# Query and key projections as 512-column products, and thirteen low parts by DMAs issued with their negation

## The chip, the cores and the metric

The kernel runs on one core of one Trainium2 chip. The core has TensorE (PE in the profile; PEld is its weight load), VectorE (DVE), ScalarE (ACT), GpSimd (POOL) and the queues that issue DMAs, above all SyncE's (SP) and GpSimd's. The metric is the device time of one execution in microseconds; of several runs the median counts.

## The reference

One layer of a hybrid decoder trunk on 256 rows of width 1024, in float32:

```python
n = _rmsnorm(h, norm_mix_g[l])
z = n @ w_in[l]
c_a, c_g, q, k, v, qi, ki, wi, gc_logit, ga_logit = _split_cols(z, IN_SIZES)
g_conv = jax.nn.sigmoid(gc_logit + bg_conv)
g_attn = jax.nn.sigmoid(ga_logit + bg_attn)
y_conv = _conformer_conv(c_a, c_g, conv_w[l], conv_b[l], conv_ln_g[l], conv_ln_b[l], w_conv_out[l])
y_attn = _dsa_attention(qh, kh, vh, qih, ki, wih) @ w_attn_out[l]
h = h + (g_conv * y_conv + g_attn * y_attn) @ w_mix_out[l]
h = h + _cross_attention(_rmsnorm(h, norm_x_g[l]), _rmsnorm(mem, norm_mem_g[l]), wx_q[l], wx_kv[l], wx_o[l])
hf = _rmsnorm(h, norm_ffn_g[l]) @ w_ff1[l]
h = h + jnp.square(jax.nn.relu(hf)) @ w_ff2[l]
return _rmsnorm(h, norm_final_g)
```

`_conformer_conv` multiplies one projection by the sigmoid of another, convolves each of 1024 channels with 31 causal taps, applies layer norm and silu, and projects. `_dsa_attention` has 8 heads of 128; an indexer of 8 small heads picks 64 keys for each query.

## The kernel before, in words

**Precision.** Each float32 operand is split into a high part, rounded to the matmul's type fp32r, and a low part, the rest. A product is made of three: high with high, high with low, low with high. For the weights the split happens in the kernel: a chunk `raw` of 128 x 2048 is loaded by SP, ScalarE copies each half (128 x 1024) to `hi`, and VectorE subtracts to give `lo`. For some second halves the low part is made otherwise: ScalarE writes minus `hi` into `lo`, and a DMA issued by POOL adds `raw` to it (`low_by_dma`, line 181).

**The stream.** The list `STREAM` fixes the order in which weight chunks are loaded and used: conv 0 to 3, the indexer's qi and ki, conv 4 to 7 (chunks 7 to 10), the gates gc and ga (11 to 18), v (19 to 22), q and k in turn (23 to 30), xk and xv of the cross attention (31 to 34), then ao (attention output, 35 to 38), co (conv output), mix, xq, xo, and the feed-forward f1 and f2. There are six buffers each of `hi` and `lo` and three of `raw`.

**Half tiles.** `form_b` handles one chunk as two half tiles of 128 output channels. A half tile has 8 steps over the input. In the narrow form a step is three products of 256 columns. In the wide form (`is_wide`, line 287) the high part of the weights multiplies both parts of the rows at once, 512 columns, and the low part multiplies the high rows, 256 columns, into the second half of the same PSUM bank; the two halves have to be added at the end. `merge` (line 319) does this: ScalarE copies the second half out, VectorE adds the first. `copy_out` (line 329) is a plain copy on ScalarE for a narrow half tile and a merge for a wide one: at once for k (`now=True`), as a chain for the others.

**Chains, ticks, fill.** Work beside the products is written as Python generators. `tick()`, called after each half tile, moves every started chain on by one `yield`, so a `yield` puts the next part of a chain behind the next half tile in the engines' orders. The 31 taps of each of 8 conv channel tiles (`acc`) wait in the list `fill`; `tick` emits taps as long as the planned cost of VectorE's work is more than 1000 below the planned cost of PE's. So what else VectorE is given in a stage sets how many taps stand there.

**The norm of the conv branch.** When all taps of all 8 tiles are emitted, `layer_norm` (line 622) is started. POOL adds up the tiles (`usum`). PE forms the mean (`ps_mub`), VectorE subtracts it, ScalarE squares, PE and POOL make the reciprocal root (`ps_vr`, `rs_vr`, `ps_rsb`), and then, pair by pair of channel tiles, VectorE scales, ScalarE applies silu, and VectorE splits into `u_p`, one pair for a tick. Before the co products, `finish(norms[0])` drains what is left. The co products read `u_p`.

**Heads.** A head's chain (`head`, line 667) begins one tick after its k half tile: scores `ps_s` on PE, mask and maximum `att_t` on VectorE, exponential on ScalarE, transposes `ps_pt` and output `ps_o` on PE, split into `o_p`.

Of the kernel before, what the change touches and what calls it, by code (L numbers as in the profile page):

```python
# [8 lines left out]
F32 = mybir.dt.float32  # L9
# [3 lines left out]
ALU = mybir.AluOpType  # L13
# [20 lines left out]
STREAM = (  # L34
    [("conv", i) for i in range(4)]
    + [("qi", i) for i in range(2)]
    + [("ki", 0)]
    + [("conv", i) for i in range(4, 8)]
    + [("gc", i) for i in range(4)]
    + [("ga", i) for i in range(4)]  # L40
    + [("v", i) for i in range(4)]
    + [(n, i) for i in range(4) for n in ("q", "k")]
# [69 lines left out]
def block_kernel(ctx, tc, x, xt, mem, memt, wst, wki, vecs, convw, gout, out):  # L112
    nc = tc.nc
# [14 lines left out]
    def t8(name, dt=F32, shape=(P, KT, S)):  # L128
        return big.tile(list(shape), dt, tag="t8", bufs=12, name=name)

    def parts_t8(name, nkt=KT):
        return Parts([t8(f"{name}{c}", F32R, (P, 4, 2, S)) for c in range(nkt // 4)])

    def w2(name, dt=F32, shape=(P, 512)):
        return work.tile(list(shape), dt, tag="w2", bufs=8, name=name)
# [10 lines left out]
    def ps_aux(name):  # L146
        return bank("aux", 2, name)
# [13 lines left out]
    def load(parts=1):  # L161
        if nload[0] >= len(STREAM):
            return
        c = nload[0]
        nload[0] += 1
        key = STREAM[c]
        raw = t8(f"raw{c}", F32, (P, N_CHUNK)) if c in EARLY else raws.tile([P, N_CHUNK], F32, tag="raw", name=f"raw{c}")
        n = KT * NK if key[0] == "ki" else N_CHUNK
        src = wki if key[0] == "ki" else wst[INDEX[key]]
        for q in range(parts):  # L170
            ns = slice(q * n // parts, (q + 1) * n // parts)
            nc.sync.dma_start(raw[:, ns], src[:, ns])
        if key in WHOLE:
            whole[key] = raw.rearrange("p (k n) -> p k n", k=2 * KT)
            return
        parts = 1 if key[0] == "ki" else 2
        for q in range(parts):
            ns = slice(q * n // parts, (q + 1) * n // parts)
            high_jobs.append(lambda ns=ns, q=q, last=q == parts - 1: high(key, c, raw, ns, q, last))

    def low_by_dma(key, c, q):

        return q == 1 and c % 3 == 2 and 8 <= c < STREAM.index(("ao", 1))

    def high(key, c, raw, ns, q, last):
        n = ns.stop - ns.start
        hi = highs.tile([P, N_CHUNK // 2], F32R, tag="hi", name=f"hi{c}_{q}")[:, :n]
        lo = lows.tile([P, N_CHUNK // 2], F32R, tag="lo", name=f"lo{c}_{q}")[:, :n]
        act(hi, raw[:, ns], AF.Copy)  # L189
        by_dma = low_by_dma(key, c, q)  # L190
        if by_dma:
            act(lo, hi.bitcast(F32), AF.Copy, scale=-1.0)

        def low():
            if by_dma:
                nc.gpsimd.dma_start(lo.bitcast(F32), raw[:, ns], accum_op=ALU.add)
            else:
                dve.tensor_tensor(out=lo, in0=raw[:, ns], in1=hi.bitcast(F32), op=ALU.subtract)
            prepared[(*key, q)] = (hi, lo)
            if last and c not in EARLY:  # L200
                load()

        low_jobs.append(low)
# [82 lines left out]

    def is_wide(kind, ct):

        return kind in ("f1", "gc", "ga", "ao", "xk") or (kind == "mix" and ct < 6) or (kind == "co" and ct < 6)

    def form_b(kind, i, x2, after, ps_of=ps_mm):

        for ct in range(2):
            w = weights(kind, i, ct, KT)
            split_ahead()
            ps = ps_of(f"ps_{kind}{i}{ct}")
            wide = is_wide(kind, 2 * i + ct)
            tile_b(ps, w, x2, wide=wide)
            after(2 * i + ct, ps if wide else ps[:, :S])
            tick()  # L300

    def form_b_late(kind, i, x2, after, cuts=(KT - 1,), ps_of=None):

        ws, banks = [], []
        held[0] = 2
        for ct in range(2):
            ws.append(weights(kind, i, ct, KT))
            split_ahead()
            banks.append((ps_of or ps_mm)(f"ps_{kind}{i}{ct}"))
            tile_b(banks[ct], ws[ct], x2, range(cuts[0]), is_wide(kind, 2 * i + ct))  # L310
        for lo, hi in zip(cuts, (*cuts[1:], KT)):
            for ct in range(2):
                tile_b(banks[ct], ws[ct], x2, range(lo, hi), is_wide(kind, 2 * i + ct))
        for ct in range(2):
            after(2 * i + ct, banks[ct] if is_wide(kind, 2 * i + ct) else banks[ct][:, :S])
            tick()
        held[0] = 1
# [64 lines left out]
    def rsqrt(sums, name):  # L382

        ps = ps_aux(f"ps_{name}")
        for rb in range(2):
            pe.matmul(ps[:, 2 * rb : 2 * rb + 2], sums[:, rb * P : rb * P + P], onesd[:, :2], start=True, stop=True)
        ms = small.tile([P, 2], F32, tag="ms", name=f"ms_{name}")
        dve.tensor_scalar(ms, ps[:, :4].rearrange("p (r t) -> p r t", r=2)[:, :, 0], EPS, None, ALU.add)
        return power(ms, name)

    def spread(cols, name):

        ps = ps_aux(f"ps_{name}")
        for rb in range(2):
            pe.transpose(ps[:, rb * P : rb * P + P], cols[:, rb : rb + 1].to_broadcast([P, P]), ident)
        return ps[:, :S]
# [65 lines left out]
    def tap(t, s):  # L462
        def go():
            j = TAPS - 1 - s
            if s == 0:
                act(acc[:, t, :], u[:, t, :], AF.Identity, scale=cw[:, t, j : j + 1], bias=cvb[:, t : t + 1])
            else:
                dve.scalar_tensor_tensor(out=acc[:, t, s:], in0=u[:, t, : S - s], scalar=cw[:, t, j : j + 1],
                                         in1=acc[:, t, s:], op0=ALU.mult, op1=ALU.add)
            if s == TAPS - 1:  # L470
                done.append(t)
                if len(done) == KT:
                    norms.append(start(layer_norm()))
                if len(done) > 1:
                    nc.gpsimd.tensor_tensor(out=usum, in0=usum if len(done) > 2 else acc[:, done[0], :],
                                            in1=acc[:, t, :], op=ALU.add)
        return go
# [143 lines left out]

    def layer_norm():
        u2.append(parts_t8("u_p"))
        yield
        mub = ps_aux("ps_mub")[:, :S]
        pe.matmul(mub, onesd, usum, start=True, stop=True)
        mub = mub.unsqueeze(1).to_broadcast([P, 2, S])
        vs = w2("vs", F32, (P, 2, S))
        pairs = [slice(2 * c, 2 * c + 2) for c in range(4)]
        for c, cs in enumerate(pairs):  # L630
            dve.tensor_tensor(out=acc[:, cs, :], in0=acc[:, cs, :], in1=mub, op=ALU.subtract)
            sq = vs if c == 0 else w2(f"sq_vr{c}", F32, (P, 2, S))
            act(sq, acc[:, cs, :], AF.Square)
            if c > 1:
                dve.tensor_tensor(out=vs, in0=vs, in1=before, op=ALU.add)
            before = sq
        waiting[0] = True
        yield
        waiting[0] = False
        dve.tensor_tensor(out=vs, in0=vs, in1=before, op=ALU.add)  # L640
        dve.tensor_tensor(out=vs[:, 0, :], in0=vs[:, 0, :], in1=vs[:, 1, :], op=ALU.add)
        yield
        rs = rsqrt(vs[:, 0, :], "vr")
        yield
        while len(headed) < NH:
            yield
        act(table, table, AF.Silu)
        rsb = spread(rs, "rsb").unsqueeze(1).to_broadcast([P, 2, S])
        for c in range(5):
            if c < 4:  # L650
                dve.tensor_tensor(out=acc[:, pairs[c], :], in0=acc[:, pairs[c], :], in1=rsb, op=ALU.mult)
                for t in (2 * c, 2 * c + 1):
                    act(acc[:, t, :], acc[:, t, :], AF.Silu, scale=lng[:, t : t + 1], bias=lnb[:, t : t + 1])
            if c > 0:
                parts_of(2 * c - 2)
            yield

    def parts_of(kt):
        hi, src = u2[0].high(kt, 2), acc[:, kt : kt + 2, :]
        dve.tensor_copy(hi, src)  # L660
        dve.tensor_tensor(out=u2[0].low(kt, 2), in0=src, in1=hi.bitcast(F32), op=ALU.subtract)
# [44 lines left out]
    def qk(name):  # L706
        return big.tile([P, 2, S], F32, tag="qk", bufs=4, name=name)

    for i in range(4):
        q, k = qk(f"q{i}"), qk(f"k{i}")  # L710
# [441 lines left out]
```

## Time and profile before

| | us |
|---|---|
| median of 3 runs (515.99 to 517.21) | 516.72 |
| the profiled execution | 516.69 |
| its span, first to last instruction | 514.9 |
| busy: PE, DVE, ACT, POOL | 503.6, 421.6, 305.3, 27.8 |

The profile is one execution. PE's busy time counts matmuls that overlap as one stretch, so it does not say how fast the stream of products runs: for that, the time of a known number of products is read from the chain of waits. Almost all PE and DVE instructions are recorded at line 77 (a helper that counts cost), so groups are told apart by their tiles: `lo<-raw,hi` is a low part, `acc<-u,cw,acc` a tap, `ps_q`, `ps_k` and so on the half tiles. The TensorE clock granted was 0.998 on the mean.

### The profile page before, as it was taken

The numbers are of one execution on the slowest core, as the hardware profiler recorded it, in microseconds if no ns is written. First come the engines' busy times: TensorE is split into PE (matmuls) and PEld (weight loads), VectorE is DVE, ScalarE is ACT, GpSimd is POOL, SyncE is SP. The second block draws the span as 40 slices with busy tenths as digits, with TensorE's granted clock in tenths as the row PEclk, the third lists the DMA queues.
The fourth block names the chain that finished last, engine by engine and source line by source line (L and its number), as shares of the span: only waits on it lengthen the run. The fifth ranks groups of instructions, "written<-read, shape, count | busy, mean of one in ns | idle before, by whom it ended". The sixth has DMA issues, their size and how long they took to land.

```text
span 514.9 us, 8076 instructions
## 1 busy us (share of the span) xinstructions
PE 503.6 (98%) x3098; PEld 448.6 (87%) x3098; DVE 421.6 (82%) x822; ACT 305.3 (59%) x523; POOL 27.8 (5%) x40
## 2 busy tenths in 40 slices
PE   8999999999999999999999999999999999999995
PEld 6999998888899999888788998988888888888884
DVE  4998999999988999999989976796766566666565
ACT  5667666677556766748557657565644454544442
POOL 2001011101021000030000000000000000000000
PEclk9999999999999999999999999999999999999999
DMA  8946555766964644464646442546445554455402
GB/s 306 367 180 237 167 169 197 253 205 204 286 241 129 204 165 129 168 188 172 241 169 240 169 164 87 200 166 243 164 174 224 215 204 163 165 176 215 182 0 81
DMA packets 15750, 97.97 MB, mean 190 GB/s; under 512 B 1744, under 2 KB 2640, under 8 KB 5216
## 3 DMA queue, kind: packets, MB, share of 16 engines
q1 hardware_dynamic: 13952, 91.85, 48.7%
q0 software_dynamic: 1472, 5.28, 5.3%
q8 instruction: 24, 0.39, 0.3%
q10 hardware_dynamic: 288, 0.33, 0.2%
q14 instruction: 14, 0.11, 0.1%
HBM read 91.16 MB, written 1.05 MB: 179 GB/s over the span
## 4 chain that ended last, share of the span: by engine, by line
PE 74%; issue 10%; DVE 9%; DMA 4%; ACT 1%; POOL 1%; SPq 0%; POOLq 0%; DVEq 0%; ACTq 0%
PE ps_f L77 17%; PE ps_ff L77 16%; PE ps_k L77 4%; PE ps_q L77 4%; PE ps_mix L77 4%; PE ps_ga L77 4%; PE ps_v L77 4%; PE ps_co L77 4%; PE ps_conv L77 3%; DVE acc L77 3%; DVE lo L77 3%; PE ps_xo L77 3%; DMA raw<-in_wst_dram 2%; PE ps_xq L77 2%; PE ps_qi L77 2%
## 5 line engine op out<-in xcount | busy, mean ns | idle before, releaser
L77 DVE TENSOR_TENSOR lo<-raw,hi 128x1024 fp32r<-128x1024 f32 x153 | 184.9, 1220 | 3.7 <-ACT hi L189 2.2
L189 ACT ACTIVATE hi<-raw 128x1024 fp32r<-128x1024 f32 x163 | 168.6, 1047 | 5.2 <-DMA raw<-in_wst_dram 3.7
L77 DVE SCALAR_TENSOR_TENSOR acc<-u,cw,acc 128x235 f32<-128x235 f32 (+22 forms) x240 | 99.9, 472 | 0.5
L77 PE MATMUL ps_f<-ff_p,hi 128*128 128x512 f32 x256 | 89.9, 396 | 0.0
L77 PE MATMUL ps_ff<-hi,fs 128*128 128x512 f32 (+1 forms) x256 | 80.8, 387 | 0.0
L77 PE MATMUL ps_f<-ff_p,lo 128*128 128x256 f32 x256 | 66.2, 279 | 0.0
L77 PEld LDWEIGHTS ps_ff<-hi,fs 128*128 128x128 f32 x256 | 47.9, 188 | 9.2
L77 PEld LDWEIGHTS ps_f<-ff_p,hi 128*128 128x128 f32 x256 | 46.8, 188 | 9.2
L983 ACT ACTIVATE ft<-ps_f 128x256 f32<-128x256 f32 x32 | 12.2, 382 | 66.9 <-PE ps_f L77 66.9
L77 DVE TENSOR_TENSOR ft<-ps_f,ft 128x256 f32<-128x256 f32 x32 | 13.6, 424 | 45.8 <-ACT ft L983 45.8
L77 PEld LDWEIGHTS ps_f<-ff_p,lo 128*128 128x128 f32 x256 | 48.3, 189 | 2.6
L77 PE MATMUL ps_ff<-lo,fs 128*128 128x512 f32 (+1 forms) x128 | 49.4, 386 | 0.0
L77 PE MATMUL ps_conv<-n_p,hi 128*128 128x256 f32 x224 | 40.9, 285 | 0.4 <-ACT sg L494 0.4
L77 PEld LDWEIGHTS ps_conv<-n_p,hi 128*128 128x128 f32 x224 | 34.8, 191 | 1.6 <-ACT sg L494 0.8
L77 PE MATMUL ps_conv<-n_p,lo 128*128 128x256 f32 x112 | 31.7, 283 | 0.0
L77 PEld LDWEIGHTS ps_ff<-lo,fs 128*128 128x128 f32 x128 | 24.1, 188 | 4.9
L77 PE MATMUL ps_q<-n_p,hi 128*128 128x256 f32 x128 | 24.4, 291 | 0.0
L77 PE MATMUL ps_k<-n_p,hi 128*128 128x256 f32 x128 | 23.4, 284 | 0.0
L77 PE MATMUL ps_ao<-o_p,hi 128*128 128x512 f32 x64 | 22.8, 402 | 0.0
L77 PE MATMUL ps_co<-u_p,hi 128*128 128x512 f32 (+1 forms) x80 | 22.3, 351 | 0.3 <-DVE u_p L77 0.3
L77 PE MATMUL ps_mix<-mix_p,hi 128*128 128x512 f32 (+1 forms) x80 | 22.2, 351 | 0.0
L77 PE MATMUL ps_gc<-n_p,hi 128*128 128x512 f32 x64 | 22.0, 396 | 0.0
(238 smaller groups left out, 1008.5 us busy)
## 6 DMA issues: line engine op xcount, KB each, us to landing
raw<-in_wst_dram SPq DMA_DIRECT2D x80, 1024.0 KB, 4.9
lo<-raw POOLq DMA_DIRECT2D x10, 512.0 KB, 5.8
raw<-in_wst_dram SPq DMA_DIRECT2D x4, 512.0 KB, 8.9
x_rm<-in_x_dram SPq DMA_DIRECT2D x2, 512.0 KB, 3.8
mem_rm<-in_mem_dram SPq DMA_DIRECT2D x1, 1024.0 KB, 8.4
mem_t<-in_memt_dram SPq DMA_DIRECT2D x1, 1024.0 KB, 10.3
h_t<-in_xt_dram SPq DMA_DIRECT2D x1, 1024.0 KB, 7.0
out_dram<-hg SPq DMA_DIRECT2D x4, 176.0 KB, 2.1
```

Source lines behind the costliest of these rows:

```text
L77: return fn(*args, **kwargs)
L189: act(hi, raw[:, ns], AF.Copy)
L983: act(t, ps[:, S:], AF.Copy)
```

## The change

Four edits. `is_wide` now also takes q and k, so their sixteen half tiles are of the wide form and go through `merge`. `low_by_dma` takes every even chunk from 8 to 32 instead of every third from 8 to 35: thirteen second halves instead of ten. The DMA that completes a low part is issued right after its negation, in `high`, and no longer when the turn of the low part comes, in `low`. And `layer_norm` has one more `yield` ahead of the mean product.

```diff
     def low_by_dma(key, c, q):
 
-        return q == 1 and c % 3 == 2 and 8 <= c < STREAM.index(("ao", 1))
+        return q == 1 and c % 2 == 0 and 8 <= c < 34
 
     def high(key, c, raw, ns, q, last):
...
         if by_dma:
             act(lo, hi.bitcast(F32), AF.Copy, scale=-1.0)
+            nc.gpsimd.dma_start(lo.bitcast(F32), raw[:, ns], accum_op=ALU.add)
 
         def low():
-            if by_dma:
-                nc.gpsimd.dma_start(lo.bitcast(F32), raw[:, ns], accum_op=ALU.add)
-            else:
+            if not by_dma:
                 dve.tensor_tensor(out=lo, in0=raw[:, ns], in1=hi.bitcast(F32), op=ALU.subtract)
...
     def is_wide(kind, ct):
 
-        return kind in ("f1", "gc", "ga", "ao", "xk") or (kind == "mix" and ct < 6) or (kind == "co" and ct < 6)
+        return kind in ("f1", "gc", "ga", "ao", "xk", "q", "k") or (kind in ("mix", "co") and ct < 6)
...
     def layer_norm():
         u2.append(parts_t8("u_p"))
         yield
+        yield
         mub = ps_aux("ps_mub")[:, :S]
```

The last line of `is_wide` is otherwise the same rule for mix and co. The names `u_p`, `ya`, `ga_t` in VectorE's order keep their meaning; the lines behind the edited places move up by one.

## The prediction

> **What bounds the kernel now.** I read the page's shares first, then the busy time by stretches, then the chain of waits, and last the waits and single rows at the places where the chain changes engine.
>
> ```profile
> PE 503.6 (98%) x3098; PEld 448.6 (87%) x3098; DVE 421.6 (82%) x822; ACT 305.3 (59%) x523; POOL 27.8 (5%) x40
> ...
> 142.90:202.50 59.60, 59.60 (x482) 58.79 (x481) 54.21 (x139) 39.97 (x86) 6.86 (x6) 1.00 0.58 186
> 202.50:227.50 25.00, 24.77 (x136) 21.14 (x134) 24.75 (x56) 16.15 (x32) 4.86 (x4) 1.00 0.47 148
> 227.50:252.00 24.50, 23.60 (x133) 20.09 (x133) 23.92 (x41) 18.54 (x31) 0.72 (x1) 1.00 0.47 175
> 252.00:272.80 20.80, 20.78 (x132) 18.66 (x132) 18.64 (x35) 9.47 (x18) 0.00 (x0) 1.00 0.59 226
> ```
>
> The columns after the window are its length and then PE, PEld, DVE, ACT, POOL. TensorE looks like the bound everywhere (98%). But from 202.5 to 252.0 VectorE is just as full (24.75 of 25.00, 23.92 of 24.50), and two full engines in one stretch do not tell which one sets the end. The chain does:
>
> ```profile
> 201.78 0.67 PE ps_s L77 x4
> 202.47 0.29 DVE att_t L77
> ...
> 203.32 3.39 DVE acc L77 x9
> 206.71 1.14 DVE lo L77
> ...
> 245.38 0.34 DVE ya L77
> 245.75 0.43 DVE ga_t L77
> ...
> 251.27 0.70 DVE u_p L77
> ...
> 252.02 20.74 PE ps_co L77 x131
> 272.76 22.93 PE ps_mix L77 x144
> ```
>
> It runs on PE until the scores of head 7 (201.78), changes to VectorE at 202.47, stays there for almost fifty microseconds (conv taps `acc`, low parts `lo`, merges `ya`, gates `ga_t`, layer norm) and returns to PE only when the last `u_p` of the layer norm is written, at 251.97. The wait behind it is in the rows:
>
> ```profile
> 251.29 0.38 PE L77 MATMUL ps_co<-u_p,lo 128*128 128x256 f32 x1 [0.56 <-DVE u_p L77]
> 252.02 0.73 PE L77 MATMUL ps_co<-u_p,hi 128*128 128x512 f32 x2 [0.34 <-DVE u_p L77]
> ...
> DVE att_t L77 <- PE ps_s L77: 3.9, 2, 2.5
> ```
>
> PE idles 0.90 us for `u_p`. Ahead of the attention VectorE was early: it waited 3.9 us for the scores of heads 0 and 1. So the rule for this change: before head 7, what PE saves counts; from head 7 to the last `u_p`, every instruction added on VectorE counts; after it PE counts again (20.78 busy of 20.80).
>
> **The change part by part.**
>
> *Wide products on PE.* The sixteen half tiles of q and k turn from 24 products of 256 columns into 8 of 512 and 8 of 256.
>
> ```profile
> 98.93 22.39 PE ps_ga L77 x128
> ...
> 148.85 5.76 PE ps_k L77 x48
> ```
>
> Two narrow half tiles of k took 5.76, so 2.88 each. Eight wide ones of the attention gate took 22.39, so 2.80 each, small waits included. 16 x 0.08 = **-1.3 us**, all but the last of it ahead of head 7's scores.
>
> The Trainium skill, *TensorE: Matmul & The Clock Gate*, section Back-to-back issue gap, gives N / 2.4 GHz plus about 2.5 ns from one warm matmul to the next. By it a narrow half tile would be 2.62 us and a wide one 2.60, the gain an estimated 0.3 us and the sum below 1.0 later. The trace differs: 5.76 us for 48 narrow products is 120 ns each, not 109, so the row is used.
>
> *Merges on VectorE.* A wide half tile needs its two halves added. ScalarE's copy is there in both forms, so each of the sixteen adds one VectorE addition. The nearest kind is the `ya` merge of the chain above: 0.34 in a busy stretch (its own duration is 0.42, but the next instruction starts before it ends). 16 x 0.34 = +5.4.
>
> *Low parts by DMA.* Ten become thirteen, so three subtractions leave VectorE: 3 x 1.14 = -3.4. ScalarE gets three negations, 3 x 1.06 = 3.2, in stages where it has room (39.97 busy of 59.60 in the q and k window); were that cover gone, it would be at most 3.2. VectorE's net is **+2.0** over the kernel. Where it falls decides, and that is in the order: `low_by_dma` no longer takes chunk 35, so its second half comes back to VectorE behind head 7. Counted in VectorE's order from head 7's `att_t` to the last `u_p`, the change has 37 taps for 35, 14 low parts for 13, 8 `ya` for 6 and 8 `ga_t` for 6. The tap queue is paced by planned cost; the merges take its room in the q and k tiles, so taps slide back.
>
> *The extra yield.* The mean product `ps_mub` goes one half tile later on PE. The last tap already lands a half tile later (in `ao01`, not `ao00`), so the whole norm starts two half tiles later. The place on VectorE just ahead of the `co` products (`acc<-acc,ps_rsb` scales a pair of channel tiles, `u_p` is its split, `ya`/`ga_t` belong to `ao`), before:
>
> ```order
> L77 TENSOR_TENSOR lo39_1_2852<-raw39_2686,hi39_1_2851 128x1024
> L77 CAST u_p1_2684<-acc_193 128x2x256
> L77 TENSOR_TENSOR u_p1_2684<-acc_193,u_p1_2684 128x2x256
> L77 TENSOR_TENSOR ya6_2908<-ps_ao30_2884,ya6_2908 128x256
> L77 TENSOR_TENSOR ga_t_1015<-ya6_2908,ga_t_1015 128x256
> L77 TENSOR_TENSOR ya7_2937<-ps_ao31_2916,ya7_2937 128x256
> L77 TENSOR_TENSOR ga_t_1015<-ya7_2937,ga_t_1015 128x256
> L77 TENSOR_TENSOR lo40_0_2882<-raw40_2785,hi40_0_2881 128x1024
> ```
>
> and changed:
>
> ```order
> L77 TENSOR_TENSOR lo39_1_2731<-raw39_2575,hi39_1_2730 128x1024
> L77 TENSOR_TENSOR acc_193<-acc_193,ps_rsb_2751 128x512
> L77 CAST u_p0_2597<-acc_193 128x2x256
> L77 TENSOR_TENSOR u_p0_2597<-acc_193,u_p0_2597 128x2x256
> L77 TENSOR_TENSOR ya6_2789<-ps_ao30_2765,ya6_2789 128x256
> L77 TENSOR_TENSOR ga_t_1017<-ya6_2789,ga_t_1017 128x256
> L77 TENSOR_TENSOR acc_193<-acc_193,ps_rsb_2751 128x512
> L77 CAST u_p1_2598<-acc_193 128x2x256
> L77 TENSOR_TENSOR u_p1_2598<-acc_193,u_p1_2598 128x2x256
> L77 TENSOR_TENSOR ya7_2821<-ps_ao31_2797,ya7_2821 128x256
> L77 TENSOR_TENSOR ga_t_1017<-ya7_2821,ga_t_1017 128x256
> L77 CAST u_p1_2598<-acc_193 128x2x256
> ```
>
> Both last pairs of `ya` and `ga_t` now stand ahead of the last `u_p`, and three splits of the norm instead of one come after `lo39_1`. The price of the window: 2 taps at 0.38 (3.39 for nine) = 0.75, a low part 1.14, 2 x 0.34, 2 x 0.43: **+3.4 us**. What the yield removes is a wait on PE:
>
> ```profile
> 226.53 0.40 PE L77 MATMUL ps_ao<-o_p,hi 128*128 128x512 f32 x1
> 226.76 0.28 PE L77 MATMUL ps_ao<-o_p,lo 128*128 128x256 f32 x1
> 226.87 0.40 PE L77 MATMUL ps_ao<-o_p,hi 128*128 128x512 f32 x1
> ...
> 227.52 0.70 PE L77 MATMUL ps_mub<-usum,onesd 128*128 128x256 f32 x2 [0.24 <-POOL usum L475]
> ...
> 227.86 0.59 PE L77 MATMUL ps_ao<-o_p,hi 128*128 128x512 f32 x1
> 228.29 0.40 PE L77 MATMUL ps_ao<-o_p,lo 128*128 128x256 f32 x2
> ```
>
> From a 512-column product to the next start is 0.23 (226.53 to 226.76); to `ps_mub` it was 0.65, and 0.43 at 227.86, where the low part by DMA of chunk 35 is used. That frees 0.4 + 0.2, but PE then stands at `co` and waits for `u_p` all the longer: worth nothing on the path. Uncovered, it would be 0.6.
>
> *Early issue.* The DMA is issued behind its negation instead of at its turn among the low parts. On POOL this shows as follows.
>
> ```profile
> 88.28 0.87 POOL L196 DMA_DIRECT2D lo<-raw  x1 [5.11 <-ACT lo L192]
> ...
> 222.19 0.83 POOL L475 TENSOR_TENSOR usum<-usum,acc 128x256 f32<-128x256 f32 x1 [0.77 <-DVE acc L77]
> 223.14 0.88 POOL L196 DMA_DIRECT2D lo<-raw  x1
> ...
> 217.07 1.06 ACT L192 ACTIVATE lo<-hi 128x1024 fp32r<-128x1024 f32 x1
> ```
>
> The DMA at 88.28 went out as soon as its negation let it. Only where a conv sum `usum` stands ahead in POOL's queue was there a delay: the negation ended at 218.13, the DMA went at 223.14. In the changed order that DMA is gone and DMAs stand ahead of the sums. POOL's queue for the taps' sums, before and then changed:
>
> ```order
> L196 DMA lo32_1_2361<-raw32_2118 128x1024
> L475 TENSOR_TENSOR usum_194<-usum_194,acc_193 128x256 x2
> L196 DMA lo35_1_2615<-raw35_2414 128x1024
> L475 TENSOR_TENSOR usum_194<-usum_194,acc_193 128x256
> L375 TENSOR_TENSOR rs_vr_2778<-ms_vr_2776,half_107 128x2
> ```
>
> ```order
> L193 DMA lo30_1_2086<-raw30_1882 128x1024
> L474 TENSOR_TENSOR usum_194<-usum_194,acc_193 128x256
> L193 DMA lo32_1_2259<-raw32_2054 128x1024
> L474 TENSOR_TENSOR usum_194<-usum_194,acc_193 128x256 x3
> L374 TENSOR_TENSOR rs_vr_2721<-ms_vr_2719,half_107 128x2
> ```
>
> The last three sums follow each other with no DMA between. What a DMA costs PE is bounded by its landing:
>
> ```profile
> DMA to landing us min/median/max: 4.5/5.8/7.8
> ...
> 88.28 7.78 DMA lo<-raw
> ...
> L77 PEld LDWEIGHTS ps_gc<-n_p,lo 128*128 128x128 f32 x64 | 12.0, 189 | 1.1 <-DMA lo<-raw 0.5
> ```
>
> Only the slowest landing (7.78) held PE up, for at most 0.5. Thirteen of them: from -0.5 (that wait gone) to +1.5 (three more such waits); I take -0.2, since most landings are 2 us earlier than the one that hurt.
>
> The Trainium skill, *DMA: Bandwidth & Descriptors*, section Anatomy of one DMA, fits a DMA of this path with 2.0 us plus its bytes over 436e3. For 512 KB that is an estimated 3.2 us, with which no low part would be late and this term would be -0.5, the sum 0.3 lower. The trace has a minimum of 4.5, so its own figures stand.
>
> **Sum.** Head 7's scores: -1.3 - 0.2. Window: +3.4. So the last `u_p` comes at about 253.9 instead of 251.97, and PE, with nothing to absorb it afterwards, ends 1.9 later. The profiled execution was 516.69 (span 514.9 and 1.8 around it), as good as the median of 516.72: **518.6 us**, 0.4% slower. Bounds: if VectorE also waits for the new copies of k, the head start of 1.3 is lost (519.9); if the window is 1 us less full than counted, 517.6.
>
> **The rivals.** About 0.2%, 1.0 us, can be told from no change here.
>
> *PE keeps its saving (faster).* VectorE is the bound only while its window is filled as counted. The wide tiles and the removed waits give 1.3 + 0.2 + 0.6 + the 0.9 of `u_p`, at best 3.0. It decides if the window on VectorE shrinks by 2 us or more, for instance because taps beside POOL's sums run unhindered; then about 514.7. For: PE's 98%, and VectorE's share of only 82%. Against: the unbroken run of VectorE in the chain from 202.47 to 251.97, to which 3.4 us are added. 0.15.
>
> *Draw.* If the `co` products are paced by the low parts of the following chunks rather than by the last `u_p`, only VectorE's count up to there matters. Two pairs of `ya` and `ga_t` then cancel (they only moved), and 3.4 - 1.5 = 1.9 remains, less 1.5: +0.4, so 517.1. For: VectorE has 18.64 of 20.80 there. Against: PE resumes right at `u_p` and is busy 20.78 of 20.80 from then on. 0.20.
>
> *Later still.* Scores now wait for VectorE's additions on k, and low parts land late in the gate stages. Three landings at 7.8 instead of 5.8 with 1 us of slack each, and the head start lost: 518.6 + 1.3 + 3 = 522.9 at most, about 521. For: one landing already hurt. Against: PE waits for k's scores only after a further half tile of 2.8. 0.10.
>
> *The change does not do what it says* on one point: the early issue moves hardly any DMA, as shown, so it cannot rescue the sum. It belongs to every case.
>
> **How the numbers follow.** Forecast 0.55, faster 0.15, draw 0.20, later 0.10. The likeliest is 518.6, its own range 517.5 to 519.9. To leave out no more than two in ten the range goes down through the draw and the dearer half of the faster case, to 515.0, and up to 520.6. Slower by over 0.2%: nearly all of 0.55, and 0.10: 0.63. Within: 0.20 and a little: 0.22. Faster: 0.15.
>
> **What would show it.** PE's q and k half tiles at 2.80; head 7's scores near 200.3; the chain again on VectorE from there to the last `u_p`, near 253.9; PE's wait for `u_p` grown from 0.9 to about 5 (it arrives 2.1 earlier and is released 1.9 later); `ps_mub` without a wait; `mix` beginning near 274.7 instead of 272.76. Wrong would be: a chain that stays on PE through `ao` and `co`, or a last `u_p` before 252.

## The result and the profile after

The changed kernel takes 523.09 us, median of 4 runs (522.73 to 523.99); the kernel before took 516.36 beside it (515.61 to 517.21). The ratio is 1.0132, with a 95% interval from 1.0111 to 1.0154: 1.3% slower. Forecast were 518.6 and at most 520.6. The profiled execution took 522.73, its span 520.9.

The same rows as before, now of the changed kernel: the page's shares, and busy time by stretches, cut at the same events (the columns after the window are its length, PE, PEld, DVE, ACT, POOL, the granted clock, DMA share, GB/s).

```profile
PE 505.8 (97%) x2970; PEld 443.4 (85%) x2970; DVE 424.3 (81%) x835; ACT 308.1 (59%) x526; POOL 31.4 (6%) x43
...
PEclk9999999999999999999799999999999999999999
```

```profile
203.50:228.50 25.00, 25.00 (x138) 21.54 (x137) 24.86 (x55) 15.33 (x32) 3.11 (x2) 1.00 0.54 181
228.50:256.50 28.00, 25.03 (x134) 20.36 (x132) 27.39 (x49) 18.99 (x31) 2.31 (x2) 0.94 0.50 184
256.50:278.90 22.40, 22.40 (x132) 20.08 (x132) 17.08 (x30) 9.02 (x18) 0.00 (x0) 0.92 0.34 128
```

VectorE is full from head 7's scores on, as before, and the stretch is longer. New is the clock: 0.94 and 0.92 in the last two stretches, and a 7 in the page's row of the clock, where before had 1.00 throughout. The chain of waits of the changed kernel:

```profile
76.20 10.40 DMA lo<-raw
86.64 14.00 PE ps_gc L77 x79
...
144.78 5.59 PE ps_q L77 x32
150.37 5.59 PE ps_k L77 x32
...
188.45 0.29 DVE att_t L77
...
197.71 0.35 DVE k L77
198.10 0.92 PE ps_s L77 x4
...
203.50 0.29 DVE att_t L77
...
255.75 0.70 DVE u_p L77
...
256.50 22.45 PE ps_co L77 x131
278.95 22.93 PE ps_mix L77 x144
```

It has the shape that was forecast (PE, then VectorE from head 7's `att_t` to the last `u_p`, then PE), with three differences. A low part by DMA stands in it ahead of the gate products: 10.40 us from issue to landing. Ahead of head 6's scores (198.10) the chain is on VectorE for ten microseconds, and the scores wait for the merge of their k. And the 131 co products behind the last `u_p` take 22.45 instead of 20.74. Before, the chain came to head 6's scores on PE alone:

```profile
191.27 5.76 PE ps_k L77 x48
197.02 0.33 PE ps_pt L77 x3
197.35 0.66 PE ps_s L77 x4
```

The waits of the changed kernel say the same:

```profile
PE ps_gc L77 <- DMA lo<-raw: 2.2, 1, 2.2
PE ps_co L77 <- DVE u_p L77: 2.1, 3, 0.9
...
PE ps_vr L77 <- DVE vs L77: 0.5, 1, 0.5
...
PE ps_s L77 <- DVE k L77: 0.3, 1, 0.3
```

PE waits once for a low part in gc (2.2), and the wait at the mean product (0.2 before) is gone, with a larger one of 0.5 at `ps_vr`, the norm's next product, in its place. Cut into three stages the loss adds up (starts and ends of the named instructions, read from the two traces):

| us | before | after | difference |
|---|---|---|---|
| A: first gc product to head 7's `att_t` | 126.4 | 127.8 | +1.4 |
| of it the gc products, to the first of ga | 22.7 | 24.8 | +2.1 |
| of it from the first q product to head 7's scores | 58.7 | 58.0 | -0.7 |
| B: `att_t` to the end of the last `u_p` | 49.5 | 52.9 | +3.4 |
| C: from there to the first mix product | 20.6 | 22.3 | +1.7 |

Together 6.6 before rounding; the gc products began 0.4 earlier in this execution, so mix begins 6.2 later (278.95 for 272.76). The q and k products themselves take 1.3 less; 0.7 of it is lost again where scores wait for k.

### The profile page after: what moved, and what is told of

Its sections match the earlier page's. It is cut to its first block, busy times and chain, and to the rows that moved or that the text cites. A ratio compares the mean times of both kernels' runs of the same rounds, so it can differ in the third digit from the quotient of the medians.

```text
span 520.9 us, 7845 instructions
## 1 busy us (share of the span) xinstructions
PE 505.8 (97%) x2970; PEld 443.4 (85%) x2970; DVE 424.3 (81%) x835; ACT 308.1 (59%) x526; POOL 31.4 (6%) x43
## 4 chain that ended last, share of the span: by engine, by line
PE 78%; DVE 12%; DMA 4%; issue 3%; ACT 1%; SPq 0%; POOLq 0%; POOL 0%; DVEq 0%; ACTq 0%
PE ps_f L77 17%; PE ps_ff L77 16%; PE ps_conv L77 7%; PE ps_mix L77 4%; DVE acc L77 4%; PE ps_co L77 4%; PE ps_ga L77 4%; PE ps_v L77 4%; PE ps_q L77 4%; DVE lo L77 3%; PE ps_k L77 3%; PE ps_gc L77 3%; PE ps_xo L77 3%; DMA raw<-in_wst_dram 2%; PE ps_xq L77 2%
## 5 line engine op out<-in xcount | busy, mean ns | idle before, releaser
L77 DVE TENSOR_TENSOR lo<-raw,hi 128x1024 fp32r<-128x1024 f32 x150 | 181.3, 1221 | 5.1 <-ACT hi L189 3.6
L77 PE MATMUL ps_co<-u_p,hi 128*128 128x512 f32 (+1 forms) x80 | 24.7, 378 | 0.6 <-DVE u_p L77 0.3
L77 PE MATMUL ps_q<-n_p,hi 128*128 128x512 f32 x64 | 24.0, 411 | 0.0
L77 PE MATMUL ps_k<-n_p,hi 128*128 128x512 f32 x64 | 22.6, 399 | 0.0
L77 PE MATMUL ps_ga<-n_p,hi 128*128 128x512 f32 x64 | 22.0, 396 | 0.0
## 6 DMA issues: line engine op xcount, KB each, us to landing
mem_t<-in_memt_dram SPq DMA_DIRECT2D x1, 1024.0 KB, 10.2
```

Of the source, the lines that this page charges most:

```text
L77: return fn(*args, **kwargs)
```

## The experiments

My theory had four terms: PE's wide tiles -1.3, the late landing +2.1, VectorE's window +3.4, and the clock +1.7, which drops because PE stands half idle while it waits for `u_p`. The 0.7 at the scores was not among them; with it the terms add up to the 6.6. The theory's rivals were that PE decides and the merges are hidden, that the DMAs are the whole loss, and that the slow co products have another cause than the clock. The stages of all runs in us, each of one profiled execution, and the medians:

| kernel | gc | A | B | C | median | ratio to before, interval |
|---|---|---|---|---|---|---|
| before | 22.7 | 126.4 | 49.5 | 20.6 | 516.2 to 516.5 | |
| changed | 24.8 | 127.8 | 52.9 | 22.3 | 523.09 | 1.0132 (1.0111 to 1.0154) |
| wide q and k alone | 22.4 | 124.7 | 56.0 | 22.3 | 522.49 | 1.0120 (1.0104 to 1.0137) |
| early DMAs alone | 24.9 | 129.5 | 43.2 | 24.9 | 517.64 | 1.0026 (1.0014 to 1.0038) |
| yield alone | 22.4 | 126.3 | 51.5 | 20.7 | 518.73 | 1.0051 (1.0036 to 1.0066) |
| early issue alone, ten DMAs | 22.4 | 126.1 | 49.5 | 20.6 | 516.76 | 1.0009 (1.0000 to 1.0019) |
| changed, DMAs at their turn | 26.1 | 129.2 | 52.9 | 21.9 | 524.67 | 1.0162 (1.0140 to 1.0184) |
| changed, without chunk 12 | 22.4 | 125.0 | 53.7 | 22.3 | 520.58 | 1.0083 (1.0068 to 1.0099) |
| changed, PE kept busy | 23.5 | 129.0 | 52.9 | 20.7 | 522.21 | 1.0120 (1.0105 to 1.0135) |
| without chunk 12, PE kept busy | 22.4 | 124.9 | 53.7 | 21.0 | 519.83 | 1.0072 (1.0057 to 1.0087) |
| wide, 17 later DMAs | 22.4 | 124.7 | 48.5 | 22.1 | 516.80 | 1.0012 (1.0000 to 1.0023) |
| the same with the yield | 22.4 | 124.7 | 48.9 | 20.6 | 515.00 | 0.9979 (0.9966 to 0.9992) |
| wide, 16 DMAs, with the yield | 22.4 | 124.7 | 50.0 | 20.6 | 516.13 | 0.9987 (0.9978 to 0.9997) |

**The parts alone.** First the wide form:

```diff
-        return kind in ("f1", "gc", "ga", "ao", "xk") or (kind == "mix" and ct < 6) or (kind == "co" and ct < 6)
+        return kind in ("f1", "gc", "ga", "ao", "xk", "q", "k") or (kind in ("mix", "co") and ct < 6)
```

> The kernel before with the wide form of q and k alone; low parts by DMA, their issue and the norm's yield stay as they were. Theory (four terms that add: PE's half tiles, a late landing in the gates, VectorE's window behind head 7's scores, the clock after PE's waits for u_p): PE gains 1.3 in q and k, no low part lands late (ten DMAs as before), and VectorE's order has 14 taps and 2 pairs of ya and ga_t more between head 7's att_t and the last u_p: 14 x 0.38 + 2 x 0.77 = +6.8. The last u_p at about 257.5, PE waits about 7 us for u_p in all, and the clock then drops as in the changed kernel, 131 co products in 22 or more instead of 20.7: 523.5 us (521.8 if the clock holds). Rival (PE decides, merges and taps are hidden in VectorE's idle time): 515.0, the last u_p not later than 252. Rival (the loss of the changed kernel comes from its DMAs): within 0.2% of before.

Measured: 522.49. Stage A is 1.7 shorter: the q and k half tiles take 45.95 us by their starts in this trace (47.29 before), -1.34, and gc is 0.3 shorter. From the first q product to head 7's scores the whole gain is kept (57.3 for 58.7), so here no score waits for k. B grew by 6.5 against a counted 6.8, and C by 1.6. The rival in which PE decides is out: against the 1.7 gained on PE stand 6.5 on VectorE and 1.6 behind it. The merges alone do not do this (two pairs of `ya` and `ga_t`); it is the 14 taps that they push behind head 7.

Then the DMAs: the rule for thirteen chunks and the issue in `high`, without the other two edits.

```diff
-        return q == 1 and c % 3 == 2 and 8 <= c < STREAM.index(("ao", 1))
+        return q == 1 and c % 2 == 0 and 8 <= c < 34
...
             act(lo, hi.bitcast(F32), AF.Copy, scale=-1.0)
+            nc.gpsimd.dma_start(lo.bitcast(F32), raw[:, ns], accum_op=ALU.add)
...
```

> The kernel before with the thirteen early DMAs alone; q and k narrow, no further yield. Theory: chunk 12's low part lands 10.4 us after its issue, behind a raw load that is in flight, and PE loses the same 2.1 us in the gc products as in the changed kernel. VectorE's window has 13 taps, a low part and 2 pairs of ya and ga_t less (-7.6), so PE no longer waits for u_p (0.9 gained) and the clock stays at 1.0: 516.4 + 2.1 - 0.9, about 517.6. Rival (the landing is late only together with the wide form, or for another chunk): 515.5, without a wait over 0.5 for a low part in gc. Rival (the DMAs slow PE's later stages as well): 519 or more.

Measured: 517.64, as expected. Of its waits on PE, two are for low parts, and none is for `u_p`:

```profile
PE ps_gc L77 <- DMA lo<-raw: 2.2, 1, 2.2
...
PE ps_v L77 <- DMA lo<-raw: 0.4, 1, 0.4
```

The same 2.2 at the same place, without the wide form. B is 6.3 shorter, so VectorE is out of the way and PE sets the end; stage C is then PE's own time and no longer a wait. The clock holds at 1.00 in this trace.

The yield:

```diff
         u2.append(parts_t8("u_p"))
         yield
+        yield
```

> The kernel before with the second yield of the norm alone. Theory (VectorE's window decides): one pair of ya and ga_t more stands ahead of the last u_p, +0.8, while the 0.4 + 0.2 us that PE loses at the mean product only become a longer wait at co. The last u_p at about 252.7, mix 0.8 later, 517.0 if the clock stays at 1.0 (PE would wait 2.3 in all, about as much as in the changed kernel, where the clock dropped); with the drop 518.5. Rival (the wait at the mean product is PE's, and PE decides): 515.6.

Measured: 518.73, though the clock held in the profiled execution, for which 517.0 was expected. B grew by 2.0, not 0.8. The rest is a wait of VectorE in this stretch, absent before:

```profile
DVE acc L77 <- PE ps_mub L77: 1.3, 1, 1.3
```

With the taps done, VectorE has nothing else in its order but the subtraction of the mean, and the mean now comes a half tile later. In the changed kernel two more taps and a low part fill that place, so it does not wait there. PE waited 2.0 for `u_p` in all in this execution, busy for 3.05 of 5.00 us, and its clock stayed at 1.00:

```profile
250.00:252.50 2.50, 1.17 (x4) 0.67 (x4) 2.43 (x7) 1.81 (x4) 0.00 (x0) 1.00 0.52 157
252.50:255.00 2.50, 1.88 (x10) 1.44 (x10) 2.43 (x5) 1.45 (x2) 0.00 (x0) 1.00 0.99 416
```

One of the four executions had a mean clock of 0.993 and was the longest (519.36).

The early issue with the old ten chunks (the diff is the `dma_start` line above, without the new rule):

> The kernel before with the early issue alone: the same ten chunks, each DMA issued behind its negation. VectorE's order is the same, so the window is not moved. Theory (what is late in the changed kernel is the landing of a DMA in the gate stages, because a raw load is in flight when it is issued; the issue itself moved hardly any DMA): the ten chunks as before, one landing of about 8 us, within 0.2% of before, 516.2. Rival (issuing early is what makes landings late, for it puts the DMAs beside raw loads): a wait of 1 us or more for a low part in gc, ga or v, 517.3 or later.

Measured: 516.76, a ratio of 1.0009: within 0.2%, no stage moved by more than 0.4. So the early issue as such is harmless, and as good as without effect. Alone, the wide form costs 6.3, the DMAs 1.4 and the yield 2.6; together it is 6.7, not the sum of 10.2, since the DMAs take back in B much of what the wide form puts there. That the DMAs are the whole loss is out.

**The late landing.** The changed kernel, without chunk 12:

```diff
-        return q == 1 and c % 2 == 0 and 8 <= c < 34
+        return q == 1 and c % 2 == 0 and 8 <= c < 34 and c != 12
```

> The changed kernel, but the low part of chunk 12 is made by VectorE again, so twelve DMAs. Theory: the 2.1 us for which PE waits in gc go, VectorE's window counts 3 taps and a low part as 1.1 more, head 7's att_t comes at about 201.4 and the last u_p at about 255.4; PE waits longer for u_p, so the clock drops as before it or somewhat more: 523.1 - 1.0, about 522.1. Rival (every landing beside raw loads is late, and the wait moves to chunk 14 or 16): 523.1 + 1.1 = 524.2. Rival (the gc wait is all there is to the surplus): 520.5 or less.

Measured: 520.58, below my 522.1 and at the rival's 520.5, and the stages tell why it is not that rival: C is still 22.3, so the clock's loss is untouched. What was wrong is the size of two other terms. Stage A fell by 2.8, since gc is 2.4 shorter (22.4) and PE's wait for k is gone too; B grew by 0.8 for a counted 1.1. The wait did not move to another chunk.

Is it the early issue that made the landing late? The changed kernel, but with each DMA at the turn of its low part:

```diff
             act(lo, hi.bitcast(F32), AF.Copy, scale=-1.0)
-            nc.gpsimd.dma_start(lo.bitcast(F32), raw[:, ns], accum_op=ALU.add)
...
-            if not by_dma:
+            if by_dma:
+                nc.gpsimd.dma_start(lo.bitcast(F32), raw[:, ns], accum_op=ALU.add)
+            else:
```

> The changed kernel, but each low part's DMA issued when the turn of the low part comes, as before the change. Theory (the landing is late because of the place of chunk 12 in the gate stages, beside a raw load, and the early issue moves hardly any DMA): as the changed kernel, a wait of about 2 us in gc for the same low part, 523.1 within 0.6. Rival (early issue puts the DMA beside the raw load and so makes the landing late): no wait over 0.5 in gc, 520.6.

Measured: 524.67, above the 523.1 within 0.6 that was expected, with a wait of 1.9 in gc as the theory had it. The timelines of SP and POOL show how. First the changed kernel, for chunk 10 and chunk 12 (start, duration of the issue, queue or engine):

```profile
61.31 0.33 SPq L172 DMA_DIRECT2D raw<-in_wst_dram  x1
...
64.31 0.91 POOL L193 DMA_DIRECT2D lo<-raw  x1
...
76.04 0.33 SPq L172 DMA_DIRECT2D raw<-in_wst_dram  x1
...
76.20 0.86 POOL L193 DMA_DIRECT2D lo<-raw  x1 [10.98 <-ACT lo L192]
```

The landings of these two DMAs, from the view of their tile:

```profile
DMA to landing us min/median/max: 5.6/5.6/5.6
...
DMA to landing us min/median/max: 10.4/10.4/10.4
```

And chunk 12 with the DMA at its turn, the timelines and then the row of its chain of waits:

```profile
76.86 0.33 SPq L172 DMA_DIRECT2D raw<-in_wst_dram  x1
...
81.09 0.87 POOL L196 DMA_DIRECT2D lo<-raw  x1 [0.21 <-issue]
```

```profile
81.09 6.07 DMA lo<-raw
```

A DMA that goes out 3.0 us after a load of `raw` (64.31 after 61.31) lands in 5.6; one that goes out 0.16 after it takes 10.4; one 4.2 after it takes 6.1. Counted from the first gc product (76.5 here, 75.7 in the changed kernel), the DMA at its turn goes out after 4.6 us and lands after 10.7; issued early it goes out after 0.5 and lands after 10.9. The early issue only moved the wait from POOL's queue into the DMA queues, behind the load. Some other landings fit: in the changed kernel the DMA at 198.08 went out 0.30 after a load (197.78) and took 9.4; in the kernel before the one at 88.28 went out 0.76 after a load (87.52) and took 7.8, and the one at 123.27 4.6 after a load (118.68) took 4.6. But the distance to the last load is not all of it: in the changed kernel the DMAs at 111.81 and 123.00 went out 2.9 and 3.1 after a load and took 7.5 and 7.4, with two loads ahead of each whose packets ran for 7.1 and 7.2.

The packets in the trace show which part is late: for the landing of 10.4 they start 5.1 us after the issue, when 118 of the load's 128 large packets have started, and run for 4.3; for the landing of 5.6 they start after 1.5 and run for 3.8. The thirteen traces hold 166 such DMAs. In 102 of them the packets start over 2 us after the issue, and each time at least 63 large packets of loads were under way in between. No run isolated this: a kernel with the load out of the way was not tried.

This kernel is also 1.6 us slower than the changed one. In its profiled execution gc is 1.3 longer, and the clock fell to 0.50 behind the wait of 1.92, which it had not done behind the 2.17 in the changed kernel:

```profile
85.00:87.50 2.50, 0.58 (x3) 0.30 (x2) 2.47 (x7) 1.78 (x4) 0.00 (x0) 0.94 0.06 10
87.50:90.00 2.50, 2.50 (x9) 2.21 (x9) 2.47 (x7) 1.40 (x2) 0.88 (x1) 0.50 0.61 187
```

**The clock.** The stretches around the last `u_p` in the changed kernel (window, length, PE, PEld, DVE, ACT, POOL, clock, DMA):

```profile
247.50:250.00 2.50, 2.50 (x15) 2.13 (x15) 2.43 (x5) 2.31 (x4) 0.00 (x0) 1.00 0.40 167
250.00:252.50 2.50, 1.23 (x6) 0.69 (x5) 2.43 (x5) 1.34 (x3) 0.00 (x0) 1.00 0.23 66
252.50:255.00 2.50, 1.48 (x5) 0.84 (x4) 2.43 (x6) 1.40 (x4) 0.00 (x0) 0.68 0.99 413
255.00:257.50 2.50, 2.36 (x6) 1.60 (x6) 2.46 (x5) 1.60 (x2) 0.00 (x0) 0.50 0.85 360
257.50:260.00 2.50, 2.50 (x10) 2.19 (x9) 1.22 (x2) 0.00 (x0) 0.00 (x0) 0.50 0.05 7
260.00:262.50 2.50, 2.50 (x16) 2.17 (x15) 0.53 (x2) 0.39 (x1) 0.00 (x0) 0.95 0.89 338
```

By the trace's record of the clock it falls to half at 253.41 and is full again at 260.23. In the 3.41 us up to the fall PE is busy for 1.77. At half clock 10 products run in a stretch of 2.5 us, where the next, nearly all at full clock, holds 16. By products:

```profile
257.95 0.63 PE L77 MATMUL ps_co<-u_p,hi 128*128 128x512 f32 x1
258.38 0.41 PE L77 MATMUL ps_co<-u_p,lo 128*128 128x256 f32 x1
...
260.73 0.40 PE L77 MATMUL ps_co<-u_p,hi 128*128 128x512 f32 x1
260.96 0.28 PE L77 MATMUL ps_co<-u_p,lo 128*128 128x256 f32 x1
```

A 512-column product takes 0.43 to the next start in the one and 0.23 in the other. To test the cause, twelve products of zeros were put where PE waits, four ahead of each of steps 2, 4 and 6 of the first co half tile; nothing uses their result.

```diff
+            if kind == "co" and ct == 0:
+                dummy = ps_aux("ps_dummy")
+                for lo, hi in ((0, 2), (2, 4), (4, 6), (6, cuts[0])):
+                    for j in range(4 if lo else 0):
+                        nc.tensor.matmul(dummy, zero_r[:, :P], zero_r, start=True, stop=True)
+                    tile_b(banks[ct], ws[ct], x2, range(lo, hi), is_wide(kind, 2 * i + ct))
+                continue
```

> The changed kernel with four further 512-column products of zeros ahead of steps 2, 4 and 6 of the first co half tile, twelve in all; their result is used by nothing. They stand where PE waits for the pairs of u_p. Theory (the clock drops because PE is idle for about half of the time there): PE stays busy, the clock stays near 1.0, the products of co after the last u_p keep 0.23 us from one to the next, and the last u_p is not moved: mix begins about 1.7 earlier, 521.4. If the clock drops for another reason, or the twelve products (2.6 us at 0.21) do not fit into the waits: 523 to 525. Rival (the slow stretch is not the clock but contention of PE with VectorE or ScalarE): products stay 0.42 apart, 523 or later.

Measured: 522.21. The stretches of this kernel, and the row of its chain:

```profile
252.50:255.00 2.50, 2.16 (x9) 1.40 (x9) 2.43 (x6) 1.41 (x4) 0.00 (x0) 1.00 0.73 298
255.00:257.50 2.50, 2.16 (x10) 1.46 (x10) 2.43 (x6) 2.50 (x4) 0.00 (x0) 1.00 1.01 426
257.50:260.00 2.50, 2.50 (x15) 2.18 (x16) 2.13 (x2) 0.03 (x1) 0.00 (x0) 1.00 0.21 88
```

```profile
257.33 20.87 PE ps_co L77 x132
```

The clock stays at 1.00, 132 products take 20.87, and stage C is 20.7, as before the change: 1.7 less, the term as sized. That work added to an engine makes a stage shorter leaves little room for another cause. Of the 1.7 only 0.9 show in the median. One of the four executions had a mean clock of 0.993 and took 523.36, the others 0.997 and 521.92 to 522.22, so the added products did not keep the clock up every time. In the profiled execution stage A was 1.1 longer than the changed kernel's: gc is 1.3 shorter, but there are waits for low parts in ga, v and k as well, with an order that is the same up to co. Chunk 12's low part, issued 0.16 after its load as before, landed after 8.7 here and not 10.4; how far the landings differ from one execution to the next was not measured further.

Both mends together, chunk 12 on VectorE and PE kept busy:

> The changed kernel with both mends: chunk 12's low part on VectorE, and twelve 512-column products of zeros in PE's waits ahead of co (their result is used by nothing). Run alone, the first gave 520.6 and kept a slow stretch of co products (135 in 23.67), the second 522.2 with the co products at full pace (132 in 20.87). Theory (landing and clock are separate terms that add): 520.6 - 1.5 = 519.1, of which the window on VectorE and PE's gain are what is left over 516.2. Rival (the clock term was an accident of one execution, or depends on the late landing): 520.2 to 520.8, as without the products.

Measured: 519.83, 0.75 below the same kernel without the products, where 1.5 was expected. C fell by 1.3, to 21.0; it would be 20.6, but the last four products still ran (until 255.13) when the last `u_p` was there (254.77). The gc products began 0.5 later in this execution. So the clock's term stands with the late landing gone, and the two mends together take 3.3 of the 6.7 that the change had cost. What is left against before is 3.1 in the profiled executions: the window on VectorE (+4.2) and 0.3 in C, less 1.5 in stage A.

**Keeping the gain.** If the terms are right, PE's 1.3 can be had when VectorE's window is not longer and nothing lands late: low parts by DMA for later chunks, and no second yield.

```diff
-        return q == 1 and c % 2 == 0 and 8 <= c < 34
+        return q == 1 and c in (8, 18, 20, 22, 24, 25, 26, 27, 28, 29, 30, 31, 32, 33, 34, 35, 36)
...
         yield
-        yield
```

> A version that is meant to keep PE's gain without the losses: q and k wide, no second yield, and the low parts by early DMAs moved to later chunks: 8, 18, 20, 22 and all from 24 to 36, seventeen in all, only one in the gc stage. Theory: PE keeps 1.3 in q and k, nothing lands late in gc, and VectorE's window has 3 taps, 4 low parts less for 2 pairs more (-4.6 as counted), so that the last u_p comes at about 246, ahead of PE: no wait at co (0.9) and no drop of the clock: 514.0. If one DMA in the q and k stage lands as late as chunk 12's did, 516; rival (a DMA for each chunk is late each time, or the loads of raw fall behind since each raw buffer is held longer): 518 or more.

Measured: 516.80, no gain, where 514.0 was expected. Stage A kept all of its 1.7, B is 48.5, and PE no longer waits for `u_p`. But it waits elsewhere, and in POOL's timeline one sees for what:

```profile
PE ps_mub L77 <- POOL usum L474: 2.2, 1, 2.2
```

```profile
217.53 0.87 POOL L193 DMA_DIRECT2D lo<-raw  x1
223.29 1.56 POOL L474 TENSOR_TENSOR usum<-usum,acc 128x256 f32<-128x256 f32 x1 [4.90 <-DVE acc L77]
```

The norm now starts as early as PE can ask for it, so the mean product stands ahead of ao and waits for the last conv sum. Seven of the ten executions also had a mean clock of 0.993 or 0.994 and took 516.8 to 517.95; the three with 0.997 took 515.7 to 516.2. Here the yield has something to save, so the next kernel is the same with the second yield:

> The version with wide q and k and seventeen low parts by early DMAs in later chunks, now with the second yield of the norm as well. Without it VectorE was early (4.1 us idle behind head 7's scores), but PE stood for 2.25 us ahead of the mean product, for a conv sum of POOL that ended at 224.85, and in most executions the granted clock was lower too (0.993 or 0.994 instead of 0.997). Theory: a half tile later (2.8 us) the sum is there, the wait at the mean product goes, and since u_p has room now, the later norm costs nothing: 515.7 (the one execution that kept its clock) - 2.2 = 513.5, in all executions if the clock drop came from that wait. Rival (the wait only moves on to co, as in the run of the yield alone): 515.7 to 517.

Measured: 515.00, ratio 0.9979 (0.9966 to 0.9992): faster than before, and 1.8 faster than without the yield. The wait at the mean product is gone, and only one of the twelve executions still has a mean clock below 0.995 (0.992, 517.56); that the lower clocks came from this wait fits, but none of those executions was traced. Of the 2.2 some came back at co:

```profile
PE ps_co L77 <- DVE u_p L77: 0.9, 2, 0.5
```

The result lies between my 513.5 and the rival's 515.7. VectorE and PE now reach co nearly together, and C is 20.6. A last variant has sixteen DMAs, with chunks 14 and 16 of the gate stages but not 12:

```diff
-        return q == 1 and c % 2 == 0 and 8 <= c < 34
+        return q == 1 and c in (8, 14, 16, 18, 20, 22, 24, 26, 27, 28, 29, 30, 31, 32, 34, 36)
```

> Wide q and k, the second yield, and sixteen low parts by early DMAs: chunks 8, 14, 16, 18, 20, 22, 24, 26 to 32, 34 and 36; so again without chunk 12, but with 14 and 16 of the gate stages. Theory: chunk 12 is a special place (its DMA was the only one of the gate stages that stopped PE), the others there land in time, and VectorE's window (1.5 less than before as counted, with head 7's scores 1.3 earlier) lets the last u_p come at about 249, ahead of PE: 513.5 to 514.5. Rival (any DMA of the gate stages can land late): a wait of 1 us or more in gc or ga for a low part, 515 to 517.

Measured: 516.13, ratio 0.9987 (0.9978 to 0.9997), not the 513.5 to 514.5 that were forecast. That chunks 14 and 16 land in time was right (gc 22.4). B is 50.0, a microsecond more than with seventeen (two low parts more in the window than there and three taps fewer), and one of the later DMAs stops PE in ao.

```profile
PE ps_ao L77 <- DMA lo<-raw: 0.9, 1, 0.9
```

## Why the prediction was wrong in size

The direction and the largest term were right, the sum was 4.5 us too small: about 2.3 of it from the landing, 1.7 from the clock and 0.7 from scores that wait for k.

- *Wide products, -1.3.* Right. The half tiles are at 2.80 (5.59 for two), and q and k together take 1.34 less, in the changed kernel and in the wide form alone.
- *The window on VectorE, +3.4.* Right: +3.4, `att_t` to the end of the last `u_p`. The count of the order times the durations of before also held for the wide form alone (6.8 counted, 6.5 measured). It failed where VectorE ran out of work: the yield alone (0.8 counted, 2.0 measured) and the DMAs alone (7.6 less counted, 6.3 measured), since a window is no longer a sum of durations once the engine idles in it.
- *Thirteen landings, "I take -0.2", with a bound of +1.5.* This step failed. It measured +2.1, beyond its upper end, and in one piece: a single landing. The ten landings of before were taken as a sample of the thirteen. But they are landings at given distances from a load of `raw`, and chunk 12's negation ends 0.16 us after a load is issued. In the trace of before the five that went out less than 2 us after a load took 6.5 to 7.8, the five over 3 us after one 4.5 to 5.1.
- *"The early issue moves hardly any DMA".* Wrong for chunk 12, whose DMA went out 4.1 us earlier than at its turn, but without consequence: the landings differ by 0.2. The conclusion, that it cannot rescue the sum, held (516.76 alone).
- *"PE, with nothing to absorb it afterwards, ends 1.9 later."* This step failed too. It let PE's wait for `u_p` grow and took the products behind it at their old pace. They ran at half clock until 260.2: +1.7, the term that was missing. The wait itself grew to 2.1, not to about 5, since the late landing and the waiting scores brought PE to its first co product at 249.7, 1.2 later than before and not 2.1 earlier.
- *The yield, "worth nothing on the path".* It fits this change, where `u_p` was late anyway; the changed kernel without the yield was not run. Its worth hangs on who is late: alone it cost 2.0 of window, and where VectorE was early it took away a wait of 2.2 on PE.
- *The head start of 1.3.* "If VectorE also waits for the new copies of k" stood in the prediction as a bound, with nothing in the sum. In part it came: head 6's scores wait for the merge of k, and 0.7 of the 1.3 is lost. No run isolated this term.
- *Later still, "522.9 at most, about 521".* The rival nearest to what happened, with both of its causes present: low parts did land late in the gate stages, and scores waited for k, though for 0.7 and not 1.3. The clock was not in it either.
- *Draw and faster.* Both are out. The last 131 co products begin right behind the last `u_p` (256.50), so they are not paced by low parts, and VectorE's window grew instead of shrinking.

What should have been seen: the forecast named a PE wait of about 5 us and costed it as idle time alone. In the trace of before PE's longest waits in this part are the 0.9 for `u_p`, and the clock holds beside them,

```profile
250.00:252.50 2.50, 1.60 (x8) 0.99 (x7) 2.43 (x5) 2.48 (x4) 0.00 (x0) 1.00 0.27 43
```

so for a wait that is five times as long the clock was an unknown, with no bound above, and the range should have left room for it.

## What to carry to other kernels

Count what an edit pushes into the window of the engine that sets the end: alone, the sixteen merges were dear here through the fourteen taps that they displaced. A transfer's price is that of its slot: look at which loads are under way when it is issued, since issuing it earlier only helps if it gets ahead of them. And a wait on TensorE can cost twice, once as idle time and once as slow products behind it.

## What the hardware showed

The granted clock fell to half without a long pause. The longest stop of PE ahead of the drop in the changed kernel was 1.3 us from one product's start to the next (250.13 to 251.46, idle for 0.93), in 3.41 us in which it was busy for 52%. In all thirteen traces the changes of the clock lie whole steps of 3.413 us apart: the half clock lasts two steps in the changed kernel (253.41 to 260.23) and one step each time in the kernel with the DMAs at their turn (87.20 to 90.61, 257.87 to 261.28). So a drop lasted at least one whole step here; the one at 87.20 began when the wait before it was just over.

Where the limit lies these runs do not say. Cut into these steps, the clock fell behind steps with PE busy for 39, 44, 52, 54 and 56%, and held behind others with 43, 51, 52 and 55%, so the busy share of one step does not decide it. Behind one wait of 1.92 in gc the clock fell, behind one of 2.17 at the same place it did not; the first lies within one step, the second across the end of one (86.15).

The Trainium skill, *TensorE: Matmul & The Clock Gate*, section HAM oscillation, puts its rule as no idle gaps of more than about 3.4 us, by which nothing would have happened here. The measurement differs. The Trainium skill, same page, section A second HAM failure mode, tells of a kernel in which PE's small idles between groups of products came often enough to make the clock swing; that agrees in kind with the three waits of 0.3 to 0.9 us around the drop here.

A low part's DMA that is issued closely behind a load of `raw` lands late by up to 5 us, and what is late is its start (5.1 us after the issue, against 1.5). The Trainium skill, *DMA: Bandwidth & Descriptors*, section Queues, rings and completion order, says that each DMA engine takes turns between its queues and drains a whole packet of one, typically 9 to 17 descriptors, before it switches. The trace is compatible with that: the load has 144 records, nine for each of 16 engines if they are spread evenly, so an engine's share of a load may be one such packet. No run here shows which records belong to one packet.
